# A conditioned decoder trunk on one Trainium2 core: modulation products in blocks of four, and the first loads in another order

## The chip, the cores and the metric

The kernel is one program on one core of one Trainium2 chip. The core has a matrix engine (PE, with its weight loads shown apart as PEld), a vector engine (DVE), an activation engine (ACT), a general engine (POOL) and an engine that does nothing here but issue transfers (SP). Each runs its own instructions in the order in which they stand in the program, and waits on the others through semaphores. PE can work at one of two clocks, 1.2 and 2.4 GHz; the profile shows the granted one as a share of the higher.

The metric is the device time of one execution in microseconds (us), taken as the median of several runs. A measurement of this kernel spreads over about half a percent.

## The reference

One sequence of 512 tokens of width 1024 goes through two layers, each a mixer (layer 0: forgetting attention, layer 1: latent attention) and a mixture of experts. What matters here is how each sub-layer is conditioned: one vector `c` gives, per layer, six rows of 1024 numbers (shift, scale and gate for the mixer, the same for the experts).

```python
c_act = jax.nn.silu(c)
for i in range(DEPTH):
    mod = c_act @ w_ada[i] + b_ada[i]                      # (1, 1024) @ (1024, 6144)
    sh1, sc1, g1, sh2, sc2, g2 = [m[:, None, :] for m in jnp.split(mod, 6, axis=-1)]
    h = rmsnorm(x, mix_norm[i]) * (1.0 + sc1) + sh1
    y = fox_mixer(h, ...) if i % N_MIXERS == 0 else mla_mixer(h, ...)
    x = x + g1 * y
    h = rmsnorm(x, ffn_norm[i]) * (1.0 + sc2) + sh2
    x = x + g2 * hier_moe(h, ...)
```

All is float32. The weights of the modulation are 2 x 25 MB, read once; the products themselves are small, since there is a single row on the left.

## The kernel before

**Modulation steps.** `ada(i, pair, rows)` computes two of the six rows of a layer, 2048 numbers. The contraction over 1024 is cut into 8 steps of 128 (`KC = 8`). A step needs two weight tiles of 512 KB, `ws[0]` and `ws[1]` (`ada_load`, L175), and makes four products (L201). The left side, `crep`, is `silu(c)` repeated over 32 columns, so a product fills only 32 of PE's 128 columns; product `g` writes partitions `32*g` to `32*g+31` of one PSUM tile, and so uses its own quarter of PE's columns (`tile_position=(0, 32 * g)`). Products 0 and 1 read `ws[0]`, products 2 and 3 read `ws[1]`. After each step the function yields, so that its caller can put other work between. A product leaves two records in the trace: the 160 products of `ada` are the 320 of L201.

Five such tables are made behind other work: three in layer 0's attention (`K.fox(..., [K.ada(0, 1), K.ada(0, 2), K.ada(1, 0)])`), one while layer 1's latents are projected (`mla_latents`) and one that runs on into the first projections of layer 1's attention (`mla`). They are the "fills".

**What sets the order.** Apart from layer 1's attention, whose PE order is written by hand, the instructions of every engine are put in order when the program is built, by a scheduler that plays the program forward with its own idea of durations and takes what is ready. `self.after(x)` keeps an instruction behind `x` in that order. On the chip nothing is reordered any more: an instruction that waits holds up all that stands behind it on its engine.

**Tiles.** Nearly all weights go through one ring of 8 tiles, `wraw` (`NRAW = 8`): the modulation weights, the attention's input weights, two tiles for the bias and norm rows of `ada`. A load waits until the tile's last reader is done. All these loads are issued by SP, one after the other.

**The start.** `first_load` loads `x` as four tiles `xl` of 128 rows. `mla_prep` loads four small gains that layer 1 needs and makes tables from them on DVE. `first_rows` then does three things that end together:

- Each of the four `xl` is squared and summed on ACT (`rms`, the squares going to a scratch tile `xn`), scaled by its factor on ACT into that same `xn` (two buffers), transposed on PE and copied to `xnT` on DVE.
- `ada_first` makes the shift and scale of layer 0 in two halves of 512 columns. A half has 8 weight loads of 512 KB (L227), 32 products (L229), an addition of the bias (`arows`), a transpose (L240) and a copy to the column `acol` (L242).
- With a half's column, four slices of `xnT` become `hT` (L300 to L303), split in a high and a low part, and `fox_begin` multiplies them with the input weights of the first pair of heads (L128 to L130, four row blocks of 128 tokens, 8 steps of the contraction).

The loads stand on SP in the order in which these functions were run: first half's weights, constants, two units of input weights, second half's weights, the other units. `fox_begin` keeps its second part behind the last product of `ada_first` (`self.last_ada`).

## Time and profile before

| what | value |
|---|---|
| time, median of 3 runs | 1121.67 us (1118.26 to 1123.49) |
| the profiled execution | 1118.59 us, of which 1116.8 us are the span of its instructions |
| PE busy | 989.6 us, 89% of the span |
| DVE busy | 817.6 us, 73% |
| ACT busy | 602.5 us, 54% |
| moved by DMA | 248 MB, mean 222 GB/s |
| records of the `ada` products (L201) on PE | 320, mean 604 ns each, 67.4 us of time in which at least one ran |

The span has these stages: the start to about 63 us; layer 0's attention to about 290 us; its output and its experts to about 580 us; layer 1's latents and first projections to about 690 us; its attention to about 850 us; its output and experts to the end. A wait in the rows below is written in brackets, as the idle time of the engine before the instruction and what ended it. PE's records overlap: what an instruction costs its engine is read from the distance of the starts, not from its length.

### The profile page before, as it was taken

The numbers are of one execution on the slowest core, as the hardware profiler recorded it, in microseconds if no ns is written. First come the engines' busy times: TensorE is split into PE (matmuls) and PEld (weight loads), VectorE is DVE, ScalarE is ACT, GpSimd is POOL, SyncE is SP. The second block draws the span as 40 slices with busy tenths as digits, with TensorE's granted clock in tenths as the row PEclk, the third lists the DMA queues.
The fourth block names the chain that finished last, engine by engine and source line by source line (L and its number), as shares of the span: only waits on it lengthen the run. The fifth ranks groups of instructions, "written<-read, shape, count | busy, mean of one in ns | idle before, by whom it ended". The sixth has DMA issues, their size and how long they took to land. (4 is left out here: it accounts for less than half of the span.)

```text
span 1116.8 us, 16794 instructions
## 1 busy us (share of the span) xinstructions
PE 989.6 (89%) x5298; PEld 734.8 (66%) x5298; DVE 817.6 (73%) x1918; ACT 602.5 (54%) x1318; POOL 348.3 (31%) x376
## 2 busy tenths in 40 slices
PE   3779999899989769999969999989797948999996
PEld 2567778677767746667636576778685836666753
DVE  4476776666863989988756378988864587998864
ACT  4345565455652436667543356888663326666640
POOL 0001111111223555544311006455422454544322
PEclk9889999999999769999999999999898968999998
DMA  7937545567456679999968758110315687999966
GB/s 252 297 94 243 159 169 178 174 210 236 164 204 201 217 236 277 320 332 324 364 217 304 286 155 305 39 58 24 110 58 170 233 266 224 307 319 332 375 235 227
DMA packets 135731, 248.34 MB, mean 222 GB/s; under 512 B 27676, under 2 KB 56734, under 8 KB 135638
## 3 DMA queue, kind: packets, MB, share of 16 engines
q1 hardware_dynamic: 123410, 211.74, 57.9%
q0 software_dynamic: 11648, 33.39, 9.6%
q10 hardware_dynamic: 580, 2.10, 0.5%
q8 instruction: 43, 0.70, 0.3%
q14 instruction: 50, 0.41, 0.1%
HBM read 222.63 MB, written 24.55 MB: 221 GB/s over the span
## 5 line engine op out<-in xcount | busy, mean ns | idle before, releaser
L340 POOL TENSOR_SCALAR prob<-prob,smx 128x128 f32<-128x128 f32 (+3 forms) x128 | 70.5, 553 | 293.4 <-DVE smx L339 208.4
L136 ACT CAST weh<-wraw 128x1024 fp32r<-128x1024 f32 x128 | 133.0, 1050 | 49.2 <-PE ps_s L130 41.2
L137 DVE TENSOR_TENSOR wel<-wraw,weh 128x1024 fp32r<-128x1024 f32 x90 | 137.5, 1557 | 13.5 <-ACT weh L136 13.5
L137 POOL TENSOR_TENSOR wel<-wraw,weh 128x1024 fp32r<-128x1024 f32 x38 | 93.8, 2469 | 57.9 <-ACT weh L136 36.7
L129 PE MATMUL ps_s<-wel,xTh 128*100 128x512 f32 x256 | 107.1, 418 | 3.1 <-DVE wel L137 2.4
L128 PE MATMUL ps_s<-weh,xTh 128*100 128x512 f32 x256 | 107.1, 420 | 3.0 <-ACT xTh L1264 3.0
L130 PE MATMUL ps_s<-weh,xTl 128*100 128x512 f32 x256 | 106.5, 416 | 0.0
L128 PE MATMUL ps_mm<-wqh,hTh 128*128 128x384 f32 x240 | 86.1, 359 | 4.6 <-ACT hTh L300 3.7
L130 PE MATMUL ps_mm<-wqh,hTl 128*128 128x384 f32 x240 | 84.7, 354 | 0.0
L129 PE MATMUL ps_mm<-wql,hTh 128*128 128x384 f32 x240 | 84.4, 352 | 0.0
L349 ACT CAST pth<-ps_pt 128x128 fp32r<-128x128 f32 (+3 forms) x128 | 53.2, 423 | 40.9 <-PE ps_pt L347 40.3
L201 PE MATMUL ps_ad<-wraw,crep 128*32 128x512 f32 x320 | 67.4, 604 | 6.0 <-DMA wraw<-in_w_ada_dram 6.0
L350 DVE TENSOR_TENSOR ptl<-ps_pt,pth 128x128 fp32r<-128x128 f32 (+3 forms) x128 | 60.7, 481 | 7.2 <-ACT pth L349 6.5
L1299 PE MATMUL ps_mm<-wraw,hT 128*100 128x512 f32 x128 | 65.3, 591 | 0.0
L347 PE MATMUL ps_pt<-ident,prob 128*128 128x128 f32 x320 | 57.4, 283 | 8.7 <-POOL prob L340 3.4
L1250 POOL DMA_INDIRECT xe<-hd,gi x32 | 48.1, 1502 | 52.8 <-PE ps_pt L1262 18.6
L128 PEld LDWEIGHTS ps_s<-weh,xTh 128*100 128x100 f32 x256 | 43.6, 171 | 21.5 <-issue 4.5
L129 PEld LDWEIGHTS ps_s<-wel,xTh 128*100 128x100 f32 x256 | 43.6, 170 | 19.0 <-DVE wel L137 3.5
L130 PEld LDWEIGHTS ps_s<-weh,xTl 128*100 128x100 f32 x256 | 43.2, 169 | 17.4 <-issue 3.7
L335 DVE CUSTOM_DVE_ANT_0 prob<-ps_s,negc 128x128 f32<-128x128 f32 (+1 forms) x64 | 31.1, 488 | 30.9 <-PE ps_pt L347 15.5
L128 PEld LDWEIGHTS ps_mm<-wqh,hTh 128*128 128x128 f32 x240 | 47.3, 197 | 9.0 <-ACT hTh L300 3.9
L1262 PE MATMUL ps_pt<-ident,xe 100*128 100x100 f32 x256 | 38.5, 289 | 14.7 <-DMA xe<-hd,gi 14.7
(476 smaller groups left out, 2764.2 us busy)
## 6 DMA issues: line engine op xcount, KB each, us to landing
wraw<-in_w_ada_dram SPq DMA_DIRECT2D x96, 512.0 KB, 6.2
wraw<-in_moe_w_gate_dram SPq DMA_DIRECT2D x128, 256.0 KB, 7.4
wraw<-in_moe_w_up_dram SPq DMA_DIRECT2D x128, 256.0 KB, 10.7
wraw<-in_moe_w_down_dram SPq DMA_DIRECT2D x64, 512.0 KB, 7.9
wraw<-in_fox_w_in_dram SPq DMA_DIRECT2D x64, 192.0 KB, 3.3
yd<-ye POOLq DMA_DIRECT2D x29, 400.0 KB, 7.1
negc<-cumd SPq DMA_DIRECT2D x16, 256.0 KB, 4.1
wraw<-in_fox_w_out_dram SPq DMA_DIRECT2D x8, 512.0 KB, 3.8
```

What stands on the lines that cost most here:

```text
L128: mm(out, lh, rh, start=start, stop=False)
L129: mm(out, lh, rl, start=False, stop=False)
L130: mm(out, ll, rh, start=False, stop=stop)
L136: self.nc.scalar.copy(hi, src)
L137: (eng or self.nc.vector).tensor_sub(lo, src, hi.bitcast(F32))
L201: nc.tensor.matmul(p[32 * g:32 * g + 32, :], self.crep[:, k, :], ws[g // 2][:, (g % 2) * 512:(g % 2) * 512 + 512], start=(k == 0), stop=(k ...
L340: nc.gpsimd.tensor_scalar(pr[:, :n], pr[:, :n], st[:, 2:3], 1.0, op0=OP.mult, op1=OP.mult)
L347: nc.tensor.transpose(p[:, j, :], pr[:, j * P:(j + 1) * P], self.ident)
L349: nc.scalar.copy(PT[0][sl], p[:, :i + 1, :])
L350: nc.vector.tensor_sub(PT[1][sl], p[:, :i + 1, :], PT[0][sl].bitcast(F32))
L1250: return self.nc.gpsimd.indirect_dma_start(out=xe, out_offset=None, in_=self.hd, in_offset=bass.IndirectOffsetOnAxis(ap=gi, axis=0), bound ...
L1299: nc.tensor.matmul(p, hT[:, 1, :], ws[1][:, cs], start=False, stop=True)
```

## The change

Two things are changed.

In `ada`, the four products of a step are recorded in the order 2, 3, 0, 1. The first of them (`head`) reads the second weight tile, and the other three are kept behind it and given high priority. So a step's first product waits for both tiles, and its other three follow it at once.

In the start, `ada_first` issues the 8 loads of its first half, its small rows, then (after `fox_begin` has issued its constants and the first two units of input weights) the 8 loads of its second half. Twelve of the sixteen loads go to a new tile `wa` with six buffers, so that fourteen tiles can hold modulation weights where there were eight. `fox_begin` yields once more, after its first loads. `x` is scaled in place, and its squares go to a scratch tile of half the size, `xsq`. `mla_prep` is run after `first_rows`.

```diff
@@ ada
         for k in range(KC):
             ws, nxt = nxt, self.ada_load(i, pair, k + 1) if k + 1 < KC else None
-            for g in range(4):
-                nc.tensor.matmul(p[32 * g:32 * g + 32, :], self.crep[:, k, :],
...
+            head = None
+            for g in (2, 3, 0, 1):
+                with ExitStack() as together:
+                    if head:
+                        together.enter_context(self.after(head))
+                        together.enter_context(self.tc.high_priority())
+                    mm = nc.tensor.matmul(p[32 * g:32 * g + 32, :], self.crep[:, k, :],
...
+                head = head or mm
             yield None
@@ ada_first
+        ws = []
         for half in range(2):
+            for k in range(KC):
+                w = pool.tile([P, 2, 512], F32, name="wa", tag="wa", bufs=6) if (k > 1 if half else k < 6) else \
+                    self.wraw.tile([P, 2, 512], F32, name="wraw", tag="wraw")
+                nc.sync.dma_start(w, ...)
+                ws.append(w)
             ...
+            yield None
+        for half in range(2):
             p = self.ps("pv" if half else "ad")[:, 0:256]
             for k in range(KC):
-                w = self.wraw.tile([P, 2, 512], F32, name="wraw", tag="wraw")
-                nc.sync.dma_start(w, ...)
+                w = ws[KC * half + k]
@@ first_rows
+        next(ada)
+        next(begin)
+        next(ada)
         for t in range(NT):
             xt = x[t]
-            xn = pool.tile([P, D], F32, name="xn", tag="xn", bufs=2)
+            junk = pool.tile([P, D], BF16, name="xsq")
...
-            nc.scalar.activation(xn, xt, AF.Copy, scale=r)
-            for half, p in self.transposed(xn):
+            nc.scalar.activation(xt, xt, AF.Copy, scale=r)
+            for half, p in self.transposed(xt):
@@ fox_begin
+        ws.update(enumerate(self.fox_weights(0, (0, 1))))
+        wfs = self.forget_weights(pool)
         self.fox_const()
+        yield
@@ body
-                prep = K.mla_prep(tables, K.const, nm)
-                begun = K.first_rows(nm, xs, hT, K.fox_begin(hT, nm))
+                begun = K.first_rows(nm, xs, hT, K.fox_begin(hT, nm))
+                prep = K.mla_prep(tables, K.const, nm)
```

The new lines move all later ones: L201 becomes L207, L227 and L229 become L231 and L243, L240 and L242 become L254 and L256. Since the order is made when the program is built, it changes in more places than the code does.

PE, in layer 1's latents, where the products of `ada(1, 1)` (`ps_ad<-wraw,crep`) stand between the projections (`ps_mm`) and transposes (`ps_pt`). Before:

```order
L128 MATMUL ps_mm<-wlh,xTh 128x384
L201 MATMUL ps_ad<-wraw,crep 32x512 x2
L129 MATMUL ps_mm<-wll,xTh 128x384
L130 MATMUL ps_mm<-wlh,xTl 128x384
L265 MATMUL ps_pt<-ident,oT_6503 128x128 x2
L201 MATMUL ps_ad<-wraw,crep 32x512 x2
L265 MATMUL ps_pt<-ident,oT_6503 128x128 x2
```

After, in the same place:

```order
L129 MATMUL ps_mm<-wll,xTh 128x384
L207 MATMUL ps_ad<-wraw,crep 32x512 x4
L130 MATMUL ps_mm<-wlh,xTl 128x384
L128 MATMUL ps_mm<-wlh,xTh 128x384
L129 MATMUL ps_mm<-wll,xTh 128x384
L279 MATMUL ps_pt<-ident,oT_6503 128x128 x4
```

Two pairs of products have become one block of four. Over the whole program the 160 products stood in 56 runs (31 of two, 8 of three, 7 of four, 3 of one, 7 of five to seven) and now stand in 37 (34 of four, 3 of eight). In layer 0's attention it was 30 runs, six of them longer than four, and is 22, two of eight; in layer 1 it was 16 and then 10 (one of seven), and is 8 and then 7 (one of eight).

SP, from the load of `x` (`xl`, just ahead) to the second half's weights (`ab` are the bias and norm rows, `wf`, `foxg` and `bf` constants of the attention). Before:

```order
L622 DMA mgr_157<-in_mla_q_norm_dram 128x32
L627 DMA mgc_160<-in_mla_q_norm_dram 64x1
L622 DMA mgr_170<-in_mla_k_norm_dram 128x32
L627 DMA mgc_172<-in_mla_k_norm_dram 64x1
L222 DMA ab_283<-in_b_ada_dram 64x1x256 x2
L223 DMA ab_284<-in_mix_norm_dram 64x1x256
L227 DMA wraw<-in_w_ada_dram 128x2x512 x8
L418 DMA foxg<-in_fox_q_norm_dram 128x1x1
L418 DMA foxg<-in_fox_k_norm_dram 128x1x1
L421 DMA bf<-in_fox_b_f_dram 16x1
L465 DMA wraw<-in_fox_w_in_dram 128x3x128 x2
```

After:

```order
L231 DMA wa<-in_w_ada_dram 128x2x512 x6
L231 DMA wraw<-in_w_ada_dram 128x2x512 x2
L235 DMA ab_158<-in_b_ada_dram 64x1x256 x2
L236 DMA ab_159<-in_mix_norm_dram 64x1x256
L484 DMA wraw<-in_fox_w_in_dram 128x3x128 x4
L407 DMA wf<-in_fox_w_in_dram 128x8x16
L435 DMA foxg<-in_fox_q_norm_dram 128x1x1
L435 DMA foxg<-in_fox_k_norm_dram 128x1x1
L438 DMA bf<-in_fox_b_f_dram 16x1
L231 DMA wraw<-in_w_ada_dram 128x2x512 x2
L231 DMA wa<-in_w_ada_dram 128x2x512 x3
```

The seven small loads ahead of the first half's weights are gone from there, and the small constants now stand behind the first two units of input weights, next to the second half's weights.

DVE, around the column of the second half (`acol`), with the table operations of `mla_prep` (`mt`, made from `mgr`, `mgc`, `cos` and `sin`). After:

```order
L251 SCALAR_TENSOR_TENSOR arows_440<-arows_440,ab_159 64x256
L137 TENSOR_TENSOR wql<-wraw,wqh 128x768 x2
L643 TENSOR_SCALAR mgr_590<-mgr_590 128x32
L648 TENSOR_SCALAR mgc_593<-mgc_593 64x1
L651 TENSOR_TENSOR mt_608<-cos,mgr_603 128x4x16
L652 TENSOR_TENSOR mt_608<-cos,mgr_603 128x4x16
L653 SCALAR_TENSOR_TENSOR mt_609<-sin,mgr_603 128x4x16
L654 TENSOR_TENSOR mt_609<-sin,mgr_603 128x4x16
L651 TENSOR_TENSOR mt_597<-cos,mgr_590 128x4x16
```

These ten operations stood near the start of DVE's work before; now they stand ahead of the copy to `acol` (three more of them follow, then that copy).

## Rows read from the trace of the kernel before

**Rows 1.** The page: span, the group of `ada`'s products, the loads of its weights.

```profile
span 1116.8 us, 16794 instructions
...
L201 PE MATMUL ps_ad<-wraw,crep 128*32 128x512 f32 x320 | 67.4, 604 | 6.0 <-DMA wraw<-in_w_ada_dram 6.0
...
wraw<-in_w_ada_dram SPq DMA_DIRECT2D x96, 512.0 KB, 6.2
```

**Rows 2.** Busy time by stretch: length, engines, PE's clock, DMA share, GB/s.

```profile
80.00:140.00 60.00, 59.76 (x356) 45.78 (x355) 40.94 (x138) 32.70 (x91) 8.52 (x16) 1.00 0.62 189
...
222.00:225.00 3.00, 3.00 (x13) 1.90 (x10) 0.06 (x1) 0.17 (x1) 0.00 (x0) 0.56 0.65 223
...
608.00:645.00 37.00, 37.00 (x187) 20.35 (x187) 16.38 (x56) 13.24 (x44) 0.21 (x1) 1.00 0.74 263
645.00:690.00 45.00, 44.60 (x249) 29.78 (x245) 37.11 (x124) 25.39 (x82) 14.12 (x25) 1.00 0.69 234
```

**Rows 3.** Waits from 80 to 290 us: us in total, times, longest.

```profile
ACT pth L349 <- PE ps_pt L347: 27.2, 22, 5.9
...
DVE prob L335 <- PE ps_pt L347: 14.6, 12, 5.8
...
PE ps_ad L201 <- DMA wraw<-in_w_ada_dram: 6.0, 4, 4.2
```

**Rows 4.** Order of time on PE, around one run: start, length, instruction.

```profile
95.58 0.35 PE L129 MATMUL ps_mm<-wql,hTh 128*128 128x384 f32 x1
95.76 0.34 PE L130 MATMUL ps_mm<-wqh,hTl 128*128 128x384 f32 x1
96.03 1.06 PE L201 MATMUL ps_ad<-wraw,crep 128*32 128x512 f32 x6
97.02 0.45 PE L381 MATMUL ps_s<-KH,QS 128*128 128x384 f32 x1
97.30 0.34 PE L381 MATMUL ps_s<-KL,QS 128*128 128x384 f32 x1
```

**Rows 5.** The same for a run of four products and one of seven.

```profile
162.03 1.07 PE L201 MATMUL ps_ad<-wraw,crep 128*32 128x512 f32 x8
163.03 0.45 PE L381 MATMUL ps_s<-KH,QS 128*128 128x384 f32 x1
...
250.07 1.92 PE L201 MATMUL ps_ad<-wraw,crep 128*32 128x512 f32 x14
251.92 0.39 PE L381 MATMUL ps_s<-KH,QS 128*128 128x256 f32 x1
```

**Rows 6.** The same for two runs of two products that waited.

```profile
146.06 1.05 PE L201 MATMUL ps_ad<-wraw,crep 128*32 128x512 f32 x4 [1.22 <-DMA wraw<-in_w_ada_dram]
...
221.51 1.15 PE L201 MATMUL ps_ad<-wraw,crep 128*32 128x512 f32 x4 [4.16 <-DMA wraw<-in_w_ada_dram]
```

**Rows 7.** Order of time in the start, on ACT and DVE.

```profile
18.47 1.06 ACT L256 ACTIVATE xn<-xl 128x1024 f32<-128x1024 f32 x1 [3.90 <-issue]
...
11.61 0.22 DVE L635 TENSOR_TENSOR mt<-sin,mgr 128x64 f32<-128x64 f32 x1
...
46.95 0.43 DVE L235 TENSOR_TENSOR arows<-ps_pv,ab 128x256 f32<-128x256 f32 x1 [9.07 <-PE ps_pv L229]
...
51.94 0.17 DVE L242 COPY acol<-ps_pt 128x8 f32<-128x8 f32 x1 [1.97 <-PE ps_pt L240]
```

**Rows 8.** Busy time by stretch in the start; DMA share and GB/s stand last.

```profile
9.40:13.00 3.60, 0.00 (x0) 0.00 (x0) 2.09 (x17) 1.88 (x7) 0.00 (x0) 1.00 0.54 129
13.00:23.00 10.00, 7.61 (x64) 4.29 (x64) 3.65 (x10) 4.52 (x9) 0.00 (x0) 1.00 1.04 377
23.00:32.00 9.00, 3.79 (x38) 2.23 (x34) 4.90 (x12) 4.06 (x7) 0.00 (x0) 0.96 0.54 130
32.00:45.00 13.00, 10.75 (x62) 6.96 (x66) 5.12 (x9) 3.16 (x6) 1.88 (x1) 0.64 1.04 358
45.00:55.00 10.00, 10.00 (x74) 7.95 (x67) 4.90 (x9) 4.53 (x7) 0.00 (x0) 1.00 1.14 291
```

More of the change, by code (lines that the diff above doesn't have):

```diff
@@ L199, in ada @@
             ws, nxt = nxt, self.ada_load(i, pair, k + 1) if k + 1 < KC else None
-            for g in range(4):
-                nc.tensor.matmul(p[32 * g:32 * g + 32, :], self.crep[:, k, :],
-                                 ws[g // 2][:, (g % 2) * 512:(g % 2) * 512 + 512],
-                                 start=(k == 0), stop=(k == KC - 1), tile_position=(0, 32 * g),
-                                 skip_group_check=True)
+            head = None
[5 more added lines that the diff above has]
+                    mm = nc.tensor.matmul(p[32 * g:32 * g + 32, :], self.crep[:, k, :],
+                                          ws[g // 2][:, (g % 2) * 512:(g % 2) * 512 + 512],
+                                          start=(k == 0), stop=(k == KC - 1), tile_position=(0, 32 * g),
+                                          skip_group_check=True)
+                head = head or mm
             yield None
@@ L218, in ada_first @@
         bias, norm = (pool.tile([P, 2, 256], F32, name=f"ab{u}") for u in range(2))
+        ws = []
         for half in range(2):
+            for k in range(KC):
+                w = pool.tile([P, 2, 512], F32, name="wa", tag="wa", bufs=6) if (k > 1 if half else k < 6) else \
+                    self.wraw.tile([P, 2, 512], F32, name="wraw", tag="wraw")
+                nc.sync.dma_start(w, _ap(self.io["w_ada"], k * P * 6 * D + half * 512, [[6 * D, P], [D, 2], [1, 512]]))
+                ws.append(w)
             part = lambda name, u: _ap(self.io[name], u * D + half * 512, [[256, 2], [0, 32], [1, 256]])
@@ L223, in ada_first @@
             nc.sync.dma_start(norm[64:, half, :], part("mix_norm", 0))
+            yield None
+        for half in range(2):
             p = self.ps("pv" if half else "ad")[:, 0:256]
             for k in range(KC):
-                w = self.wraw.tile([P, 2, 512], F32, name="wraw", tag="wraw")
-                nc.sync.dma_start(w, _ap(self.io["w_ada"], k * P * 6 * D + half * 512, [[6 * D, P], [D, 2], [1, 512]]))
+                w = ws[KC * half + k]
                 for g in range(4):
@@ L284, in first_rows @@
         ada = self.ada_first(pool)
+        next(ada)
+        next(begin)
+        next(ada)
         for t in range(NT):
             xt = x[t]
-            xn = pool.tile([P, D], F32, name="xn", tag="xn", bufs=2)
+            junk = pool.tile([P, D], BF16, name="xsq")
             with self.after(self.last_sin if t == 0 else None):
-                r = self.rms(xt, xn, t == 0)
-            nc.scalar.activation(xn, xt, AF.Copy, scale=r)
-            for half, p in self.transposed(xn):
+                r = self.rms(xt, junk, t == 0)
+            nc.scalar.activation(xt, xt, AF.Copy, scale=r)
+            for half, p in self.transposed(xt):
                 nc.vector.tensor_copy(xnT[:, half * 4:half * 4 + 4, t * P:(t + 1) * P], p)
@@ L428, in fox_begin @@
         f = self.ps("ad")
-        ws, wfs = {}, None
+        ws = {}
         def rows(t, ks):
@@ L438, in gates @@
                     mm(f[:48, :], wfs[:, k, :], hT[x][:, k, :], start=(k == 0 and x == 0), stop=(k == KC - 1 and x == 1))
+        ws.update(enumerate(self.fox_weights(0, (0, 1))))
+        wfs = self.forget_weights(pool)
         self.fox_const()
+        yield
         for half in range(2):
             ks = range(4 * half, 4 * half + 4)
-            ws.update(zip(ks, self.fox_weights(0, (2 * half, 2 * half + 1))))
             if half == 0:
-                wfs = self.forget_weights(pool)
                 for t in range(NFIRST):
@@ L448, in fox_begin @@
             else:
+                ws.update(zip(ks, self.fox_weights(0, (2, 3))))
                 with self.after(self.last_ada):
```

## The prediction

> **What bounds the kernel now.** I read the page first [rows 1]: the products of `ada` are 67.4 us of PE's time in 1116.8, and their group stood idle for 6.0 us only, waiting for weights. So their cost is PE's own time, if PE is what the stages that hold them wait for. The stretches say that it is: in 80 to 140 us PE is busy 59.76 of 60, DVE 40.94 and ACT 32.70, and in 608 to 645 us PE 37.00 of 37, DVE 16.38 [rows 2]. In 645 to 690 us it is closer: PE 44.60 of 45, DVE 37.11. The waits of layer 0's attention point the same way: ACT stood 27.2 us and DVE 14.6 us for PE's transposes, while the one long wait of PE is for modulation weights, 6.0 us in four pieces [rows 3]. A microsecond of PE's work taken out there should move the end, as long as something else is ready.
>
> The start has another bound. DVE waited 9.07 us for the last product of the second half, until 46.95 us, and its column came at 51.94 us [rows 7]; nothing of the rest of the first projections can end before it. The products waited for their weights: 32 to 45 us moved 358 GB/s, at a DMA share of 1.04, but before that there are two holes, 9.4 to 13 us at 129 GB/s and 23 to 32 us at 130 GB/s, where 13 to 23 us ran at 377 [rows 8].
>
> **The blocks.** What does a run of products cost PE? Read the starts [rows 4]: two products of another kind ahead of the run are 0.18 us apart, and the three instructions before and the first after the run span 95.58 to 97.30, so 1.72 us for three such steps and the run. 1.72 - 3 x 0.18 = 1.18 us for the run, of which 0.99 lies between its start and the next one's (96.03 to 97.02). That run holds three products. One of four takes 1.00 us (162.03 to 163.03), and one of two ran 1.05 us [rows 6] where that of three has 1.06 and that of four 1.07 [rows 4, 5]: products on different quarters of PE run beside each other, and a run costs the same with two as with four. A run of seven takes 1.85 us (250.07 to 251.92), 0.85 us more than one of four [rows 5].
>
> The order gives the counts. Layer 0's attention: from 30 runs, six with a second wave, to 22, two with one: 8 x 1.18 + 4 x 0.85 = 12.8 us. Latents: from 16 runs to 8, 8 x 1.18 = 9.4 us; first projections behind them: 10 to 7, one second wave in each, 3 x 1.18 = 3.5 us. Together 25.7 us of PE's time.
>
> Not all of it need reach the end, since the scheduler put these products where it had little else ready. At the upper bound all of it does (PE at 99% and more in three stretches). For the lower bound I take the busiest follower: DVE has 37.11 of 45 us in the last stretch [rows 2], and a softmax chain that PE must wait for would leave the gaps open; 40% is 10 us. I take three quarters, 19.3 us, nearer to the upper end because 27.2 and 14.6 us of waits for PE [rows 3] are there to be taken up.
>
> **The wait for two tiles.** The first product of a block now waits for the second tile, and behind it stands all of PE's queue; SP in turn waits for PE's release of the tiles before it loads the next. Before, four runs waited 6.0 us [rows 3], two of them the first of a new table: 4.16 us at 221.51 and 1.22 us at 146.06 [rows 6]. The third table's first block now stands some 50 instructions later in PE's order, at 0.18 us each 9 us, so that the 4.16 us should be covered; with it goes the low clock behind it, 0.56 over 222 to 225 us [rows 2], about 1.3 us. The second table's first block stands where it stood and waits for one tile more: one more load, 1 to 3 us, of which I take 2.5. So -4.2 - 1.3 + 2.5 = -3 us, between 0 and -5.5.
>
> **The start.** The second half's weights come to PE when all that SP issued ahead of them has been moved. The hole at 9.4 us held 3.6 x 129 = 0.46 MB, which takes 1.2 us at 377 GB/s: 2.4 us lost. The hole at 23 us held 9 x 130 = 1.17 MB, mostly in short pieces, which at the 291 GB/s of the attention weights' own stretch [rows 8] takes 4.0 us: 5.0 us lost. The first hole has the seven small loads in it that the change moves back; the second has SP waiting for ring tiles, the constants `foxg` and `bf`, and bias rows. With 14 tiles the waits for the ring should go; the constants are still between the halves. So at best 7.4 us, and 1 more if PE stops lagging (45 to 46.9 us); at worst 2.4. I take 6.5, nearer to the upper end because in the new order SP has the next large loads right behind the constants.
>
> The Trainium skill, page "DMA: Bandwidth & Descriptors", section Specifications, puts the limit of HBM at about 358 GB/s for a core. The trace has 377 GB/s over ten microseconds [rows 8], so here the measurement decides; by the page's figure the 10.5 MB of x and both halves would take 29.3 us where 377 GB/s makes 27.9, an estimate of 1.4 us less gain, and the sum would be 1094 instead of 1092.
>
> Costed at nothing: the scaling in place and the smaller scratch tile. ACT's 3.90 us before the third square [rows 7] go, since the two buffers of `xn` are no longer waited for, but the last product of the second half covers them; without that cover they would be worth up to 3.9 us. The ten table operations of `mla_prep` now stand ahead of the second `acol` on DVE, at most 0.22 us each [rows 7], 2.2 us; DVE idled 1.97 us there [rows 7], which hides them, if their four small loads, issued behind six pieces of attention weights, have landed. If not, up to 2 us are given back.
>
> **The sum.** Against the profiled execution, 1118.6 us (span 1116.8): -19.3 - 3 - 6.5 = -28.8, so 1089.8 us. The median of the runs, 1121.67, is 3.1 us above that execution; with this I come to 1093, and give 1092. All later stages, the experts' with their weight loads among them, start when the stages before them free their tiles, and should only shift.
>
> **The rivals.**
>
> *The softmax takes over.* PE's gaps stay open, because the products were fillers while DVE, ACT and POOL worked on a head. Then a third of 25.7 us arrives, 8.6, and 1118.6 - 8.6 - 3 - 6.5 + 3.1 = 1104 us. For it speaks that DVE is at 37.11 of 45 us in the last stretch [rows 2]; against it that PE's waits for anything but weights do not appear in layer 0's attention among the long ones, while others wait for PE [rows 3].
>
> *The start gains little.* The small constants between the halves leave the hole as it was, or the second half's loads wait for the six tiles: only 2.4 us or less, 1096 to 1099 us. For it speaks that the hole at 23 us [rows 8] comes where SP's old order has those constants; against it that behind them stood loads that needed tiles of the ring, and these no longer wait for it.
>
> *Slower: every block stalls PE.* A block needs 1 MB, and the ring holds two tiles until the slower of two loads has landed, 6.2 us after its issue in the median [rows 1]. The point from which it decides: 28.8 us over 37 runs, a mean wait of 0.78 us. At the 1.22 us of the second table [rows 6] on each run, 37 x 1.22 = 45 us, the time is 1137 us. Against it: only four runs waited in layer 0's attention [rows 3], the eight blocks of the latents, over 28 us, would be about 4 us apart, which asks for 1 MB in 4 us, 260 GB/s, on a stretch that moved 263 at a share of 0.74 [rows 2].
>
> *The change does not do what it says.* That would be blocks still split; the order shows none of fewer than four.
>
> **How the numbers follow.** Forecast, 1082 to 1100 us: 0.63. Softmax: 0.18. Start: 0.10 (inside the forecast's own range). Stalls: 0.05, of which 0.03 slower than before. More gain than 1082: 0.04. The range runs from 1081 (every term at its upper bound is -39.7, 1079 against the profiled execution and 1082 against the median) to 1108 (every term but the wait at its lower bound: -10 - 2.4, with no gain from the wait, 1109). About 0.5% is what a measurement can tell from no change, 5.6 us: faster by more than that has 0.93, within it 0.03, slower 0.04.
>
> **What would show it.** In the trace of the changed kernel L207 should show eight records in about 1.07 us per run, and some 37 runs; the stretch of the latents from its first to its last block should fall from 36 to about 28 us. If PE is idle between blocks, releasers on L207 tell which rival holds: weights (stalls) or none of them, with L364 waiting for POOL or L398 for DVE (softmax). No wait of 4 us at the third table. In the start the two holes should be shut, the last product should end near 40 us, and the second `acol` come near 45 us; if `mt` operations with a wait for `mgr` stand right before it, the hidden term was not hidden. The prediction is wrong as a whole if the time lies above 1108: then PE's time was not what these stages waited for.

## The result

The changed kernel takes 1110.55 us (median of 4 runs, 1106.24 to 1113.87) where the kernel before takes 1121.66 beside it: a ratio of 0.9895, with a 95% interval of 0.9866 to 0.9924. It is faster, by 11 us instead of the 29 that were forecast, and 2.5 us outside the range. Its profiled execution took 1113.87 us, the slowest of its four, and that of before, 1118.59 us, lies 3 us under its median. So the two traces differ by only 4.7 us (spans of 1116.8 and 1112.1), and a comparison of them understates the gain by some 6 us. The ratios below are all taken against the kernel before, run beside each kernel (1121.2 to 1122.4 us).

The page of the kernel after: span, busy PE and the group of `ada`'s products.

```profile
span 1112.1 us, 16807 instructions
...
PE 970.9 (87%) x5298; PEld 737.9 (66%) x5298; DVE 819.1 (74%) x1918; ACT 600.0 (54%) x1318; POOL 351.0 (32%) x376
...
L207 PE MATMUL ps_ad<-wraw,crep 128*32 128x512 f32 x320 | 44.6, 638 | 13.8 <-DMA wraw<-in_w_ada_dram 13.8
```

The products fell from 67.4 to 44.6 us of PE's time, and their waits for weights rose from 6.0 to 13.8 us [rows 1]. So the blocks are there, and something that was costed as a gain of 3 us became a loss.

Busy time by stretch after (length, PE, PEld, DVE, ACT, POOL, PE's clock, DMA share, GB/s), to be laid beside [rows 2] and [rows 8]:

```profile
9.40:13.00 3.60, 1.46 (x12) 0.43 (x16) 1.52 (x9) 3.60 (x9) 0.00 (x0) 1.00 1.05 394
13.00:23.00 10.00, 9.27 (x88) 5.20 (x80) 5.97 (x15) 4.63 (x9) 0.00 (x0) 1.00 0.95 327
23.00:32.00 9.00, 2.06 (x6) 1.34 (x6) 5.89 (x12) 4.69 (x7) 1.21 (x1) 0.67 0.51 139
...
45.00:55.00 10.00, 8.27 (x42) 5.99 (x43) 4.30 (x16) 2.57 (x4) 0.00 (x0) 0.83 0.64 162
80.00:140.00 60.00, 56.45 (x338) 45.63 (x337) 40.77 (x136) 33.17 (x93) 7.85 (x15) 0.94 0.53 166
...
608.00:645.00 37.00, 37.00 (x246) 27.30 (x245) 22.65 (x73) 17.69 (x58) 0.69 (x2) 1.00 0.85 308
645.00:690.00 45.00, 39.14 (x223) 27.94 (x222) 33.36 (x118) 23.13 (x73) 13.40 (x24) 0.92 0.70 239
```

Of the two holes in the start's transfers the first is shut (394 GB/s instead of 129). The second is as wide as it was (139 GB/s instead of 130), and a third has come, 45 to 55 us at 162 instead of 291. From 80 to 140 us PE is no longer always busy (56.45 of 60 instead of 59.76), and its clock is down to 0.94.

Three waits of the start and four in the stages behind it, in order of time:

```profile
46.73 1.08 PE L243 MATMUL ps_pv<-wa,crep 128*32 128x256 f32 x8 [4.27 <-DMA wa<-in_w_ada_dram]
...
47.88 0.42 DVE L249 TENSOR_TENSOR arows<-ps_pv,ab 128x256 f32<-128x256 f32 x1 [14.43 <-PE ps_pv L243]
...
53.89 0.17 DVE L256 COPY acol<-ps_pt 128x8 f32<-128x8 f32 x1 [1.35 <-PE ps_pt L254]
...
105.43 1.93 PE L207 MATMUL ps_ad<-wraw,crep 128*32 128x512 f32 x8 [2.57 <-DMA wraw<-in_w_ada_dram]
...
154.01 1.94 PE L207 MATMUL ps_ad<-wraw,crep 128*32 128x512 f32 x8 [4.73 <-DMA wraw<-in_w_ada_dram]
...
303.84 1.09 PE L364 MATMUL ps_pt<-ident,prob 128*128 128x128 f32 x4 [5.06 <-POOL prob L357]
...
655.76 1.94 PE L207 MATMUL ps_ad<-wraw,crep 128*32 128x512 f32 x8 [4.56 <-DMA wraw<-in_w_ada_dram]
```

The second half's last product ended at 47.8 us instead of 46.95, and its column came at 53.89 instead of 51.94 [rows 7]. The second and the fifth table's first blocks waited 4.73 and 4.56 us; each block behind one of these waits took 1.93 us where others take 1.07, at the lower clock (0.50 granted at 153 us). The wait of 2.57 us at 105.43 is in the middle of the first table. The wait at 303.84 us is of another kind: four transposes that wait for POOL's part of the last softmax stand ahead of the first output products.

The two stages with `ada`, from the first product of `ada` to the first output product (attention), and from the first to the last block (latents and first projections), PE being the first figure behind the length. Before:

```profile
81.60:301.30 219.70, 211.12 (x1253) 165.37 (x1252) 152.91 (x479) 125.41 (x332) 30.97 (x53) 0.99 0.60 190
...
608.70:689.60 80.90, 80.87 (x430) 49.66 (x429) 52.51 (x176) 38.63 (x125) 14.10 (x26) 1.00 0.71 246
```

After:

```profile
83.40:305.20 221.80, 203.42 (x1262) 167.85 (x1262) 158.01 (x491) 127.87 (x340) 36.53 (x57) 0.96 0.61 193
...
615.00:687.20 72.20, 66.67 (x414) 47.44 (x413) 48.78 (x170) 36.48 (x121) 11.52 (x22) 0.95 0.76 269
```

In layer 1 the stage became 8.7 us shorter. In layer 0's attention PE did 7.7 us less, and yet the stage became 2.1 us longer: PE's idle time in it rose from 8.6 to 18.4 us (waits for weights from 6.0 to 8.3, the wait for POOL 5.1, waits for DVE from 2.6 to 5.0), and its mean clock fell from 0.99 to 0.96.

### The profile page after: what moved, and what is told of

The parts are those of the page before. It is cut to its first block, busy times and chain, and to the rows that moved or that the text cites. A ratio compares the mean times of both kernels' runs of the same rounds, so it can differ in the third digit from the quotient of the medians.

```text
span 1112.1 us, 16807 instructions
## 1 busy us (share of the span) xinstructions
PE 970.9 (87%) x5298; PEld 737.9 (66%) x5298; DVE 819.1 (74%) x1918; ACT 600.0 (54%) x1318; POOL 351.0 (32%) x376
## 4 chain that ended last, share of the span: by engine, by line
PE 52%; DMA 19%; DVE 12%; issue 7%; SPq 4%; ACT 3%; POOL 3%; POOLq 0%; ACTq 0%; DVEq 0%
PE ps_mm L128 6%; PE ps_mm L129 6%; PE ps_mm L130 6%; PE ps_s L398 4%; DMA wraw<-in_w_ada_dram 4%; DMA xe<-hd,gi 4%; PE ps_s L129 3%; PE ps_ad L207 3%; PE ps_s L130 3%; PE ps_s L128 3%; DMA wraw<-in_moe_w_gate_dram 3%; PE ps_pv L387 3%; PE ps_pt L364 3%; PE ps_mm L1318 2%; DMA wa<-in_w_ada_dram 2%
## 5 line engine op out<-in xcount | busy, mean ns | idle before, releaser
L137 DVE TENSOR_TENSOR wel<-wraw,weh 128x1024 fp32r<-128x1024 f32 x90 | 137.9, 1557 | 19.7 <-ACT weh L136 19.3
L364 PE MATMUL ps_pt<-ident,prob 128*128 128x128 f32 x320 | 57.6, 283 | 12.8 <-POOL prob L357 7.5
L207 PE MATMUL ps_ad<-wraw,crep 128*32 128x512 f32 x320 | 44.6, 638 | 13.8 <-DMA wraw<-in_w_ada_dram 13.8
L1328 POOL DMA_DIRECT2D yd<-ye x29 | 17.6, 606 | 123.6 <-DVE ye L1319 71.5
L364 PEld LDWEIGHTS ps_pt<-ident,prob 128*128 128x128 f32 x320 | 40.2, 145 | 21.4 <-POOL prob L357 10.0
```

The costliest lines, as they stand in the source:

```text
L137: (eng or self.nc.vector).tensor_sub(lo, src, hi.bitcast(F32))
L207: mm = nc.tensor.matmul(p[32 * g:32 * g + 32, :], self.crep[:, k, :], ws[g // 2][:, (g % 2) * 512:(g % 2) * 512 + 512], start=(k == 0), st ...
L364: nc.tensor.transpose(p[:, j, :], pr[:, j * P:(j + 1) * P], self.ident)
```

## The two parts apart

`e1_blocks` has only the change in `ada`, `e2_start` only that of the start.

> Only the blocks of four: ada as in the kernel after, the start as in the kernel before. If the two parts of the change add up, and the start lost 1.9 us (second acol at 51.94 us before, 53.89 after), the blocks alone take 1121.7 - 11.1 - 1.9 = about 1109 us. A rival theory, that the blocks lose what they gain because the new start hands them its delay, expects more: the sum of the prediction without its start, 1121.7 - 22.3 = about 1099 us. In the trace: the latents' stretch from first to last block at 26 us in both; long waits at the first blocks of the second and fifth table if these belong to the blocks.

> Only the start: the loads' order, the six more tiles, x scaled in place, mla_prep after first_rows; the products of ada in the old order. If the start lost in the trace of after what it shows there, second acol at about 54 us and a time of 1122 to 1124 us, no faster than before. If the 1.9 us were an accident of that execution and the start gains as predicted, second acol at 45 us and 1115 us.

Measured: blocks alone 1113.45 us, a ratio of 0.9932 (0.9905 to 0.9958); start alone 1123.15 us, 1.0019 (1.0001 to 1.0038), over 12 runs, with its second `acol` at 53.67 us. So the start lost about 2 us (0.1 to 4 by the interval), and the later column is no accident of one execution. The blocks brought 8 us; the two make some 6 together, and the kernel after gained 11, so the parts add up only within some 5 us. The theory that the start's delay eats the blocks' gain is out: it asked for 1099 us.

## Rows that go through two DMA engines

What is late? In 150 to 154 us after, PE stood still for the second table's tile, and the transfers had not stopped; they ran at a ninth of the full share. Most of the 56 packets that started there are of 4 KB, the size of the weights' own pieces; a row's piece has 2 KB. They are the tail of the weight loads:

```profile
150.00:154.00 4.00, 0.00 (x0) 0.02 (x1) 2.00 (x8) 0.77 (x3) 0.00 (x0) 0.81 0.11 43
```

The same share stands in the first hole of the kernel before, where almost nothing but the bias and norm rows (`ab`, pieces of 1 KB, 31 of the 33 packets) was on its way:

```profile
10.30:11.00 0.70, 0.00 (x0) 0.00 (x0) 0.54 (x5) 0.35 (x3) 0.00 (x0) 1.00 0.13 45
```

0.13 of sixteen DMA engines is two. The loads of `ab` read `[[256, 2], [0, 32], [1, 256]]` in the start and `[[512, 4], [0, 32], [1, 512]]` or `[[512, 2], ...]` in `ada`: two or four source rows, each repeated for 32 partitions. Three such loads of a half are 192 pieces of 1 KB; at 45 GB/s they take about 4.4 us, an estimate from that row. A weight load is spread over all sixteen engines (a share of 1.04 where only such loads ran [rows 8]), so my reading is that each one queued behind the rows waits for its part on the same few engines; the two experiments below put it to the test. The Trainium skill, page "DMA: Bandwidth & Descriptors", section "Why a DMA increments its semaphore by 16 and not by 1", states the rule: a load is dealt to the largest number of engines, up to 16, that divides the slowest dimension of both its sides. The trace agrees, 0.13 with a dimension of two.

Two experiments load the same bytes as pieces of 32 partitions with one source row each, so that the slowest dimension is 32; `e3_spread_first` in `ada_first`, `e6_spread_ada` in the five tables.

```diff
-        nc.sync.dma_start(bias, _ap(self.io["b_ada"], ..., [[512, 4], [0, 32], [1, 512]]))
+        for g in range(4):
+            nc.sync.dma_start(bias[32 * g:32 * g + 32], _ap(self.io["b_ada"], ... + g * 512, [[0, 32], [1, 512]]))
```

> The kernel after, but the bias and norm rows of ada_first are loaded in pieces of 32 partitions with one source row each (six loads a half instead of three), no byte more or less. Theory A: a load of rows whose source has an outer dimension of two goes through two of the sixteen DMA engines (DMA share 0.13 in 10.3 to 11.0 us of before and 0.14 in 25.5 to 26.7 us of after), and every weight load queued behind it ends late for these two engines' sake. Then each half's rows no longer hold up those two engines for some 5 us: no wait of 1.44 and 0.96 us of DVE for ab in the first half, the last weight load of the second half lands 4 us earlier (46.7 to about 42 us), second acol at 48 to 50 us instead of 53.9, and the time falls by 3 to 5 us below after, to 1105 to 1107. The Trainium skill, page DMA: Bandwidth & Descriptors, section Why a DMA increments its semaphore by 16 and not by 1, gives this rule. Theory B: the last load is late because its wa tile is released late by PE; then second acol stays within 1 us of 53.9, and the time within 1 us of after or above it, for three more issues a half on SP.

> The kernel after, but the bias and norm rows of ada (the five tables, not ada_first) are loaded in pieces of 32 partitions with one source row each (four and two loads instead of one and one). Theory A (the rows go through four and two of sixteen DMA engines, and the weights queued behind wait for these engines): the waits of the first blocks of the second and fifth table (4.73 and 4.56 us in after) fall to under 2 us, the half clock behind them goes, and the time is 5 to 9 us below after, 1102 to 1106. Theory B (a block waits long because it needs two tiles and the ring frees them late): the waits stay within 1 us of 4.7 and 4.6, the time within 2 us of after.

In 25.5 to 26.7 us of after, which the first expectation names, the packets are of 512 bytes, those of the attention weights: the low share there is the delay behind the rows and not the rows themselves.

`e6_spread_ada`: 1101.05 us, 0.9823 (0.9799 to 0.9847), 9.5 us below after by the medians, 8 by the ratios. Its PE, at the places of the waits at 105.43 and 154.01 us:

```profile
105.42 1.06 PE L210 MATMUL ps_ad<-wraw,crep 128*32 128x512 f32 x8 [2.50 <-DMA wraw<-in_w_ada_dram]
...
150.03 1.07 PE L210 MATMUL ps_ad<-wraw,crep 128*32 128x512 f32 x8 [1.94 <-DVE rsvq L147]
```

The second table's block comes 4 us earlier and at the full clock, with a wait of 1.94 us left, and the fifth table's wait is gone. The wait at 105.43, in the middle of a table with no rows ahead of it, stays: all six kernels with blocks in the attention and the start's column in its old place have it, 2.3 to 2.9 us long, and the five without blocks there have not, so it comes with the blocks and not with the rows. From 60 to 420 us PE's order is that of after, instruction for instruction, so this is not another order; the attention takes 6.9 us less (221.80 in after), and the stretch in layer 1 66.2 us instead of 72.2:

```profile
83.50:298.40 214.90, 201.25 (x1263) 167.40 (x1262) 157.68 (x491) 128.18 (x340) 36.45 (x57) 0.98 0.64 199
```

Theory A holds for the tables.

`e3_spread_first`: 1109.44 us, 0.99 (0.9876 to 0.9924), no more than 1 us below after, where 3 to 5 were expected. But the mechanism worked; the gain was lost behind it:

```profile
41.97 0.42 DVE L250 TENSOR_TENSOR arows<-ps_pv,ab 128x256 f32<-128x256 f32 x1 [10.18 <-PE ps_pv L244]
...
48.43 0.18 DVE L644 TENSOR_SCALAR mgr<-mgr 128x32 f32<-128x32 f32 x1 [1.63 <-DMA mgr<-in_mla_q_norm_dram]
...
49.64 0.16 DVE L257 COPY acol<-ps_pt 128x8 f32<-128x8 f32 x1
```

The second half's products end 5.9 us earlier (41.9 instead of 47.8), the column only 4.25. Its transposes stand behind some 30 products on PE (46.48 us), and `mla_prep`'s operations, which DVE must pass first, now wait for their own loads. In the second hole, 23 to 32 us, this kernel moves 219 GB/s where after moves 139, with the small constants where they were. From 150 to 740 us this execution is 7 to 12 us ahead of after's trace; at the end it is 5. Where the rest went stays open.

`e7_before_spread_ada` and `e8_blocks_spread_ada` do the same to the tables' rows with the start of before: without and with blocks. `e4_spread_all` has the rows of both places in pieces.

> The kernel before, with the bias and norm rows of the five tables of ada loaded in pieces of 32 partitions (as in e6_spread_ada), nothing else. Theory A, the rows on few DMA engines delay the weights behind them in every version: the 6.0 us of PE's waits for these weights in layer 0's attention fall to about 2, with 1 to 2 us of low clock, so 1121.2 - 5 = about 1116 us. Rival A2, the rows hurt only where a block asks for two tiles: 1120 to 1122 us.

> e1_blocks (the start of before, blocks of four) with the rows of the five tables loaded in pieces of 32 partitions. If the blocks are worth what the prediction's sum says (22.3 us with the two-tile wait) once the rows no longer delay the weights, 1121.2 - 22.3 = about 1099 us; in the trace no wait above 2.5 us at a table's first block, the attention of layer 0 at least 10 us shorter than before, the latents 10 us. If the 9.5 us between after and e6_spread_ada came from an interplay with the new start, less: e1_blocks - 3 or so, 1110 us. Its distance to e7_before_spread_ada is what blocks of four are worth without the rows' delay: by the prediction's lower bound 10 us, by its value 19.

> The kernel after, with the rows of ada_first and of the five tables loaded in pieces of 32 partitions. If the 4.3 us by which the second acol came earlier in e3_spread_first reach the end: 1101 - 4 = 1097 us. If they are given back behind (e3_spread_first was only about 1 us faster than after, though its first half of the program was 8 us ahead), 1100 to 1101 us. Second acol again near 49.6 us, held there by the order on PE (the transposes of arows stand behind some 30 products) and on DVE (mgr ahead of acol).

Measured: 1105.98 us (0.985, 0.9818 to 0.9882), 1102.20 (0.9823, 0.9787 to 0.9859) and 1100.19 (0.9795, 0.9755 to 0.9835). Rival A2 is out: the kernel before gains 16 us from an edit of its rows' loads, more than from the whole change. Its own 6.0 us of waits in layer 0's attention fell to 1.0, and the third table's 4.16 us [rows 6] were among them:

```profile
PE ps_ad L204 <- DMA wraw<-in_w_ada_dram: 1.0, 1, 1.0
```

That, with the low clock behind the longest of them (1.3 us in the prediction), could be some 6 of its 16 us, but the trace does not show them at the stage's end: the attention takes 219.80 us in `e7_before_spread_ada` and 219.70 before, with another order on PE from 213 us on. The whole trace, of an execution of 1109.9 us, is 8.7 us shorter than that of before, in pieces of 1.5 to 2.8 us over all its stages but the attention. Where the 16 us come from stays open. `e4_spread_all` came out at its second case, 1 us under `e6_spread_ada` (3 by the ratios, with overlapping intervals).

The blocks, with the rows out of the way, are worth only 4 us between these two, far below the 10 of the lower bound. Their stages say otherwise. The attention and the stretch in layer 1, without blocks and then with them:

```profile
80.10:299.90 219.80, 212.50 (x1274) 169.09 (x1273) 161.52 (x500) 128.49 (x344) 36.66 (x58) 0.97 0.61 198
604.60:682.90 78.30, 78.30 (x423) 48.52 (x422) 50.75 (x173) 37.86 (x124) 14.13 (x26) 1.00 0.72 250
```

```profile
83.40:296.10 212.70, 199.42 (x1262) 164.92 (x1262) 157.53 (x490) 128.19 (x340) 36.55 (x57) 0.98 0.65 201
604.40:670.70 66.30, 64.15 (x412) 45.66 (x411) 50.93 (x169) 37.01 (x121) 12.49 (x23) 1.00 0.82 294
```

That is 7.1 us less in the attention and 12.0 in layer 1: 19.1 in all, close to the 19.3 of the forecast. But 9 us come back in the stages that hold no product of `ada` (304.7 to 308.3 us between the two, 425.2 to 430.8 behind), and 3 ahead of the first product. What gives them back is not shown. PE's work in the attention is 13.1 us less, and two reasons why the stage saved only 7 can be read off: waits for weights rose from 1.0 to 5.6 us, and `e8_blocks_spread_ada` has the 5.1 us wait for POOL at the attention's end, `e7_before_spread_ada` has not. It is in all six kernels that have blocks in the attention and the column in its old place (after, `e1_blocks`, `e3_spread_first`, `e4_spread_all`, `e6_spread_ada`, `e8_blocks_spread_ada`), and in none of the others.

## The column of the second half

`e9_spread_all_col` is `e4_spread_all` with the column's way cleared: the other products are kept behind its transposes, and `mla_prep` behind the last `hTl`. `e13_start_only_fixed` has this and the start's rows in pieces, `e14_column_only` this alone.

```diff
                 with self.after(self.last_ada):
                     gates(range(4))
+                with self.after(self.last_turn):
                     for t in range(NFIRST, NT):
                         rows(t, range(4))
...
-                prep = K.mla_prep(tables, K.const, nm)
+                with K.after(K.last_low):
+                    prep = K.mla_prep(tables, K.const, nm)
```

> e4_spread_all, and in the start the second half's column is taken out of the queues: the transposes of arows stand right behind the first gates on PE, ahead of the other products, and the operations of mla_prep on DVE behind the last hTl. Theory: in e3_spread_first the products of the second half ended at 41.9 us, but the column came at 49.6 us, since the transposes stood behind 33 products (46.5 us) and acol behind a wait of 1.63 us for mgr. Then acol comes at 44 to 46 us, as the prediction had it, the 2.4 us of PE's wait for hTh go, and the time is 2 to 4 us below e4_spread_all, 1093 to 1098 us. Rival: PE's own work up to 65 us sets the end of the first projections, and the column's place moves nothing: the same time as e4_spread_all within 1 us.

> The kernel after with the rows of ada_first in pieces and the second column taken out of the queues (as in e9_spread_all_col), while the rows of the five tables stay as they are in after. It prices the start alone: second acol at about 45 us instead of 53.9, as the prediction had it. Theory: 1110.6 - 8.4 = about 1102 us, the start's term of the prediction (-6.5) instead of the +1.9 that after showed. Rival: the experts' stages give it back, and it lies within 3 us of after.

> The kernel after with the second column taken out of the queues (as in e13_start_only_fixed), while the rows of ada_first are loaded as in after. It completes the square of the start: after 1110.6, rows in pieces alone (e3_spread_first) 1109.4, both (e13_start_only_fixed) 1098.0 us. Theory: the two delays stand one behind the other, the last product at 47.8 us for the rows' sake and the column 6 us behind it for the order's; so the column alone comes at 50 to 51 us instead of 53.9, and the time is 1110.6 - 3.5 = about 1107 us, with the rest of the 12.6 us only where both are done. Rival: the column's place carries all of it, and the rows of ada_first nothing: about 1098 us.

Measured: `e9_spread_all_col` 1091.54 us, 0.9718 (0.9681 to 0.9756); `e13_start_only_fixed` 1097.99, 0.9796 (0.9772 to 0.9819); `e14_column_only` 1099.95, 0.9809 (0.9774 to 0.9845). The second column in `e13_start_only_fixed`, and then in `e14_column_only`:

```profile
41.44 0.42 DVE L250 TENSOR_TENSOR arows<-ps_pv,ab 128x256 f32<-128x256 f32 x1 [9.68 <-PE ps_pv L244]
...
44.15 0.16 DVE L257 COPY acol<-ps_pt 128x8 f32<-128x8 f32 x1
```

```profile
48.16 0.42 DVE L249 TENSOR_TENSOR arows<-ps_pv,ab 128x256 f32<-128x256 f32 x1 [14.61 <-PE ps_pv L243]
...
52.14 0.17 DVE L256 COPY acol<-ps_pt 128x8 f32<-128x8 f32 x1 [1.99 <-PE ps_pt L254]
...
292.96 0.44 PE L398 MATMUL ps_s<-KH,QS 128*128 128x384 f32 x1 [0.86 <-DVE smx L352]
```

`e9_spread_all_col`, with its column at 45.28 us, lies 8.7 us below `e4_spread_all`, where 2 to 4 were expected; `e13_start_only_fixed` lies 4 us below its theory. With both edits, the column comes at the 45 us that the prediction named. With its place alone it comes 1.75 us earlier than after, and still the time is 10.6 us lower (9.6 by the ratios). The theory on that run falls; the rival's time came (about 1098 us), but not by its reason, since the column hardly moved. Its trace shows where the time went instead: the edit gave the attention another order (the first product of `ada` runs 9.4 us earlier, at 74.0 us), and at the attention's end the output products no longer stand behind the last softmax; the longest wait there is 0.86 us instead of 5.06. The first output product comes at 294.2 us instead of 305.2. So of the 12.6 us between after and `e13_start_only_fixed` only a part is the start's. Between `e14_column_only` and `e13_start_only_fixed`, which differ in the start's rows alone, the traces keep 8 us from 60 us to the end, but the medians differ by 2; `e14_column_only` has executions at 1099.9 and at 1105, and the traced one is of the upper kind. How much the start is worth stays between these.

## Is PE's time what the attention waits for?

`e10_blocks_layer1` is `e9_spread_all_col` with blocks in layer 1's two tables alone, `e11_no_blocks` without any.

> e9_spread_all_col with the blocks of four only in the two tables made in layer 1 (latents and first projections); the three tables of layer 0's attention have the products in the old order again. Theory: with the rows out of the way the blocks pay where PE is what the stage waits for; the attention is 7 us longer without them (219.8 us from its first product of ada to its first output product in e7_before_spread_ada, 212.8 in e8_blocks_spread_ada), so 1091.5 + 7 = about 1098 us. Rival: what the blocks save in the attention is given back behind it (its last softmax and the experts' stage), as the 3.8 us between the medians of e7 and e8 suggest: 1091 to 1093 us.

> e9_spread_all_col with all products of ada in the old order: the start and the rows' loads are kept, the blocks are undone. Theory: the blocks are worth 7 us in the attention and 12 in latents and first projections, so 1091.5 + 19 = about 1110 us. Rival, by the medians of e7 and e8: 1091.5 + 4 = about 1095 us. Between the two: one of the two stages gives its gain back; then it is within 2 us of e10_blocks_layer1 (the latents' share) or 12 us above it (the attention's).

Measured: 1090.19 us, 0.9729 (0.9709 to 0.9749), and 1104.13 us, 0.9837 (0.9815 to 0.986). So the blocks are worth 13.9 us in layer 1 and about nothing in the attention: the rival on `e10_blocks_layer1` holds, and on `e11_no_blocks` the case between the two, in which the attention gives its gain back. Latents and first projections, with blocks and without:

```profile
595.10:663.00 67.90, 65.81 (x412) 46.50 (x411) 51.06 (x169) 37.06 (x121) 13.80 (x26) 0.97 0.81 292
```

```profile
595.10:673.40 78.30, 78.30 (x423) 48.53 (x422) 50.74 (x173) 37.84 (x124) 14.10 (x26) 1.00 0.72 251
```

Of the 13.9 us these stages show 10.4; the rest arises behind them.

That the attention gave nothing could mean that PE does not set its end, or that the blocks lose there what they save. To tell these apart, PE was given more to do: the first block of each table is recorded several times, each time starting its sums anew, 12 blocks more in the attention (`e15_more_attention`) or in layer 1 (`e16_more_latents`), with no load added. `e17_again` is `e9_spread_all_col` on the same chip.

```diff
+            for again in range(5 if k == 0 and (i, pair) not in ((1, 1), (1, 2)) else 1):
                 head = None
                 for g in (2, 3, 0, 1):
```

> e9_spread_all_col with the first block of each of the three tables made in layer 0's attention recorded five times (each starts its sums anew, so the output is the same): 12 more blocks, at 0.99 us from one block's start to the next 11.9 us more of PE's time, and no more loads. Theory A (PE's time in that stage does not set the end): at most 3 us more than e17_again. Theory B (PE's time does set it, and the blocks lost their 10.5 us there by their own waits for two tiles): 9 to 12 us more.

> e9_spread_all_col with the first block of each of the two tables made in layer 1's latents and first projections recorded seven times: 12 more blocks, 11.9 us more of PE's time, in the stage where the blocks were worth 13.9 us (e10_blocks_layer1 against e11_no_blocks). Theory: PE is what this stage waits for, so 9 to 12 us more than e17_again. Rival (the 13.9 us came from elsewhere, the order behind it): under 4 us more.

> e9_spread_all_col once more, so that the two kernels with added blocks, and e10_blocks_layer1 through the kernel before, have it from the same chip: 1091.5 us within 2 us.

Measured: 1100.55 us (0.9794, 0.9757 to 0.9831), 1092.92 (0.9763, 0.9738 to 0.9789) and 1087.56 (0.9702, 0.9678 to 0.9726). By the ratios the added blocks cost 10 us in the attention and 7 in layer 1, by the medians 13 and 5. In layer 1 the theory asked for 9 to 12 and the rival for under 4; the repeated blocks stood one behind another there and added 9.0 us to PE's work, not 11.9, and 7.8 to the stage (75.6 us instead of 67.8). In the attention my theory A falls, with every execution at least 4.9 us above the median of `e17_again`: more work on PE does reach the end. How much of it does is less sure, since two of the six executions of `e15_more_attention` took 1092.5 us and four 1099 to 1103, and since PE's order in this stage is another than in `e17_again`. The attention in `e10_blocks_layer1`, `e17_again` and `e15_more_attention`, one after the other:

```profile
63.50:284.90 221.40, 218.74 (x1307) 174.19 (x1307) 160.69 (x504) 131.23 (x347) 32.57 (x53) 0.99 0.62 193
```

```profile
66.50:279.60 213.10, 207.12 (x1303) 172.31 (x1303) 158.63 (x493) 126.62 (x340) 30.57 (x53) 0.99 0.63 199
```

```profile
66.10:293.20 227.10, 219.38 (x1399) 175.18 (x1399) 159.17 (x493) 128.99 (x342) 33.70 (x53) 0.99 0.60 187
```

With the 12 blocks PE has 12.3 us more to do, and the stage is 14 us longer. The blocks of four take 11.6 us off PE's work (218.74 to 207.12), and 3.3 us come back as idle time (2.7 to 6.0); the stage becomes 8.3 us shorter. It begins 3.0 us later, so its end moves by 5.3, from 284.9 to 279.6. Behind 300 us 2 to 4 of these are left, and at the end 2.7 in the traces, 3 by the ratios (0.9702 against 0.9729), with the intervals overlapping. `e17_again` beats both kernels of this study, 34 us below before; `e10_blocks_layer1` is within its spread.

## Why the prediction was wrong, step by step

**What bounds the kernel: right, as far as it was tested.** Of 12.3 us of work added to PE in the attention 10 to 13 came out at the end, of 9.0 in layer 1 5 to 7. The first of these runs had another order on PE as well.

**The price of a run and the counts: right.** 37 runs, eight records in 1.07 us. (The rows give two instructions ahead of the run and one behind it, not three and one; the 1.18 us stand.) Without long waits for weights PE's work falls by 11.6 us in the attention (`e10_blocks_layer1` to `e17_again`), where 12.8 were reckoned. Latents: first to last block 26 us instead of 36, where 28 was forecast. In layer 1 the two stretches' 12.9 us are 8.7 in the trace of after (with 5.5 us of its own waits in them) and 10.4 to 12.0 where nothing delays them (`e10_blocks_layer1` against `e11_no_blocks`, `e8_blocks_spread_ada` against `e7_before_spread_ada`).

**"I take three quarters": wrong for the attention, right for layer 1.** Of 12.8 us there PE's work shows 7.7 less in the trace, and none of it reached the stage's end. The step that failed is the reason given: that others wait for PE [rows 3] says that saved time would be used, not that the new order makes no waits of its own. It made three: the second table's wait for weights, which `e6_spread_ada` cut from 4.73 to 1.94 us; the 2.57 us at 105.43, which come with the blocks and stay; and the wait of 5.06 us for POOL at the attention's end, which the traces show but no run isolates. Without the rows' delay the attention becomes 7 to 8 us shorter with blocks, not far from the forecast's share of 9.6; where it was 8.3 (`e17_again` against `e10_blocks_layer1`), the program's end showed 3. The rival of the softmax, 1104 us, named the right kind of place but the wrong mechanism: the gaps between the blocks were filled, and the softmax cost PE 5 us at the stage's end, in one instruction.

**The wait for two tiles: wrong in sign.** -3 us were forecast; the waits rose by 7.8 us, and with each of the three long ones the clock fell. The third table's 4.16 us did go, as forecast. The second table's wait, put at 2.5 us more, rose from 1.22 to 4.73. The fifth table's 4.56 us and the 2.57 at 105.43 were put at nothing, and they are most of the miss. The failed step is "one more load, 1 to 3 us": it priced the second tile as a load on free engines, while its part on two of the sixteen stood behind the rows. With the rows in pieces the waits in the attention are 4.0 us (the forecast's terms make 4.3 of them), none is left in layer 1, and the time is 8 to 9.5 us lower. The wait at 105.43 is not of this cause. The trace of before had the evidence: the first hole [rows 8] was read as "seven small loads in it" and costed by its bytes, 0.46 MB, where a narrower stretch inside it shows the share of 0.13, two engines at work.

**The start: wrong in sign.** -6.5 us were forecast, about +2 came. The first hole shut, as said. The second did not, since the same rows of `ab` now stand behind each half's weights, ahead of the next loads (with them in pieces, 219 GB/s instead of 139); and the last weight load stands behind the second half's rows (issued at 35.27 us, used at 46.73). The rival "the start gains little" had the small constants as its cause; they stand in the same place in `e3_spread_first`, where the last product ends 5.9 us earlier, so they were at most a small part.

The start's miss (8.5 us) and that of the rows (8 to 9.5) make up the 18.6 us between 1092 and 1110.55 nearly whole. That they do so this well is in part luck: see the last point.

**Costed at nothing:** scaling in place held, ACT's 3.90 us [rows 7] are gone. `mla_prep` was hidden in after (the column waited 1.35 us for PE behind it), but not where the column came early: 1.63 us for `mgr` in `e3_spread_first`.

**"All later stages should only shift": roughly.** From the first output product to the latents' first block it took 307.4 us before, 309.8 after, 304.7 in `e7_before_spread_ada` and 312.5 in `e17_again`, with the same code. So "only shift" does not hold to better than this. Each edit gives the scheduler another order, and stages that no edit touches move by several microseconds. Differences between two of these kernels that are smaller than that have no cause that this study shows; that is why the parts do not add up better.

## What to carry to other kernels

Read a hole in the transfers by its DMA share, not only by its bytes: here 0.13 was two engines of sixteen, and weight loads queued behind 192 to 384 KB of such rows came 4 to 6 us late. Load a repeated row so that its slowest dimension is the 32 copies and not the two or four rows; that edit alone took 8 to 9.5 us off the kernel after, at PE's same order through the attention, and 16 off the kernel before, where the order changed too. And when instructions are tied into blocks, look for the stage's seams (first block of a table, end of the stage) before counting the work saved: here what was saved all along the attention was lost in four waits. Compare two kernels stage by stage, too: the blocks saved 19 us in their own stages and 4 at the end.

## What the runs showed that was not expected

With weight loads in place of the seven small ones, 9.4 to 13 us moved 394 GB/s at a DMA share of 1.05, above the 377 of before's best stretch of [rows 8].

A wait of 2.5 to 5 us can cost more than its length. Behind each of the three in after the block took 1.93 us instead of 1.07, and behind the one at 105.43 the products ran 0.32 us apart instead of 0.17 until 111.3 us, at a granted clock of 0.50:

```profile
107.78 0.52 PE L129 MATMUL ps_mm<-wql,hTh 128*128 128x384 f32 x1
108.10 0.52 PE L130 MATMUL ps_mm<-wqh,hTl 128*128 128x384 f32 x1
```

It need not: in `e1_blocks` a wait of 2.92 us at the same place left the block at 1.06 us and the clock at 1.00 to 108 us. What decides between the two is not shown.

```profile
103.67 1.06 PE L206 MATMUL ps_ad<-wraw,crep 128*32 128x512 f32 x8 [2.92 <-DMA wraw<-in_w_ada_dram]
```
